# Three edits to the selective scan of a two-layer hybrid network on one core: transposing products, a folding product, and the place of the decay products

## Chip, cores and metric

One core of one Trainium2 chip. The metric is the device time of one execution in microseconds (us); three executions of the kernel before took 1320.59, 1317.4 and 1319.07 us, median 1319.07 us. Everything is float32 or a float32 split into two parts that TensorE takes in its faster float32 form.

## The reference, cut to what matters

A network of two layers works on 512 tokens (the latent stream) and 256 context tokens, 1024 channels each. Each layer normalises and modulates its input, projects it, and feeds three mixers in parallel: an attention, a long convolution and a selective scan (SSD), whose outputs are gated, joined, projected back and normalised. The second layer needs the context only as far as the latent stream reads it.

The change is inside the scan. It runs in both directions over chunks of 128 tokens, for 8 heads of 64 channels in 2 groups of 4, with a state of 128 numbers per channel. In one chunk and one direction:

```
acs      = cumsum(dt * a)                         # dt: softplus(projection + bias), per head
decay_ls = exp(acs[l] - acs[s])  for s <= l       # 128 x 128 per head
y_diag   = sum_s  (C[l] . B[s]) * decay_ls * dt[s] * x[s]
y_off    = (C[l] . state at the chunk's start) * exp(acs[l])
y        = y_diag + y_off  (both directions added)  + x * d_skip
```

## The kernel before, in words

The kernel is one long program. A scheduler in the compiler lays down a fixed order for each engine, taking ready instructions by the order in which they were written; on the chip each engine then follows its list, and waits where a semaphore tells it to. Work of different stages is therefore mixed in the list of TensorE: while the scan runs, the blocks of the input projection (`proj`, lines 450 and 452; a block is 128 output channels, and its weights come through two buffers `wr` and are split on ScalarE and VectorE, lines 170 and 171) and of the modulation (line 359) are its other work. In layer 0 the order of the steps is "V, S, 1, P, 2, G" and in layer 1 "S, V, 1, P, 2, G": `S` is `ssm_in`, `P` is `ssm`, the other letters are projections for the long convolution.

`ssm_in` (lines 669 to 759) projects x, B, C and the step sizes dt. The projection of dt is made with its weights' high and low parts side by side, so the result `dr` has 32 rows: 16 high, 16 low. Lines 704 and 705 make it, with stationary operands of 32 columns. Lines 707 to 711 then turn it round, tokens onto partitions, into `pd`: for each of 6 chunks two products with a part of the identity, the second added to the first, so that high and low parts are summed. VectorE's line 718 reads `pd` and begins a chain of small instructions to dt, its cumulative sums (lines 738 to 745), and `rd`, two rows per head in DRAM.

`ssm` (lines 761 to 845) first runs the states from chunk to chunk (`scan`, lines 772 to 792), then goes over the chunks, six in layer 0 and four in layer 1. For a chunk:

- line 798: B times C for both groups, copied by ScalarE to `gm` (line 800); lines 805 and 807 find what a token adds to itself (`own`).
- lines 810 to 819: `ys`, on VectorE: x times `own`, plus for either direction the product of C with the state (line 816, into `po`) times its decay. Tokens are on the partitions.
- line 821: four products of 128 columns each, `ys` as the stationary operand and the identity as the moving one: `ys` transposed, into the accumulator `py`, whose bank they open.
- lines 823 to 842, for each group: a tile `R` of 512 KB is loaded from `rd`, broadcast to all partitions (line 825); six bias instructions of ScalarE (line 833) and two of VectorE (line 831); a predicated copy (line 835); an exponential (line 836); and line 838, which multiplies with `gm` into a tile `M` of its own. Then four products (line 842), one per head, add the group's decay part to `py`.
- line 843 copies `py` to `bc`, line 844 stores it.

`R` has three buffers, `M` two. A buffer of `R` comes free with line 838, and that of `M` with line 842. All the loads and stores named here are issued from SyncE's queue (SP), in one order. PSUM has five banks `wk` for these products.

Of the kernel before, what the change touches and what calls it, by code (L numbers as in the profile page):

```python
# [9 lines left out]
F32 = mybir.dt.float32  # L10
# [8 lines left out]
P = 128  # L19
# [16 lines left out]
# columns of the per-layer parameter block  # L36
C_HCW, C_SCW, C_NW, C_BM = 0, 48, 80, 84
NPAR = 108
# columns of the constant block
K_ID, K_U, K_L, K_ONE = 0, 128, 256, 384  # L40
NCON = 512
# blocks of 128 columns of w_in
# [3 lines left out]
class Net:  # L46
    def __init__(self, ctx, tc, a):
        self.tc, self.nc, self.a = tc, tc.nc, a
        nc = self.nc
        self.one = ctx.enter_context(tc.tile_pool(name="one", bufs=1))  # L50
        self.dr = ctx.enter_context(tc.tile_pool(name="dr", bufs=1, space=DRAM))
        self.ps = ctx.enter_context(tc.tile_pool(name="ps", bufs=1, space=PSUM))
        self.sb = ctx.enter_context(tc.tile_pool(name="sb", bufs=1))
        self.n = 0
        self.kd = {}
        self.th = {}
        self.ph = None
        self.rr = 0

        self.ml = self.tq([P, 4, 768])  # L60
        fw = self.ml[:, 3]
        self.fw = fw
        nc.sync.dma_start(self.ml.rearrange("p a b -> p (a b)")[0:33, 1536:2432], a["mlp1"])
        self.cc = self.one.tile([P, 16], F32, name="cc")
        nc.sync.dma_start(self.cc, a["cc"])
        nc.sync.dma_start(fw[:, 128:392], a["mlp2"])
        self.row = self.one.tile([P, DEPTH, 48], F32, name="row")
        nc.sync.dma_start(self.row, a["row"].partition_broadcast(P))
        self.con = self.one.tile([P, NCON], F32, name="con")
        nc.sync.dma_start(self.con, a["con"])  # L70
        self.ident = self.con[:, K_ID:K_ID + P]
        self.par = self.one.tile([P, DEPTH, NPAR], F32, name="par")
        nc.sync.dma_start(self.par, a["par"].rearrange("l p n -> p l n"))
        self.identb = self.one.tile([P, P], BF16, name="identb")
        nc.vector.tensor_copy(self.identb, self.ident)
        self.maskb = self.one.tile([P, 2, P], BF16, name="maskb")
        mk = self.ip("V", [P, QW])[:, :2 * P]
        nc.sync.dma_start(mk, a["mask"])
        nc.vector.tensor_copy(self.maskb.rearrange("p a b -> p (a b)"), mk)
        self.upper = self.one.tile([P, P], mybir.dt.uint8, name="upper")  # L80
        nc.vector.tensor_copy(self.upper, self.con[:, K_U:K_U + P])
        gc = self.one.tile([P, 512], F32, name="gc")
        self.gc = gc.rearrange("p (q s k) -> p q s k", q=2, s=2)
        self.mhalf = self.one.tile([P, 16], F32, name="mhalf")
        nc.vector.memset(self.mhalf, -0.5)
        for l in range(DEPTH):
            s = self.par[:, l, C_SCW:C_SCW + 32]
            nc.vector.tensor_scalar_mul(s, s, 0.5)
        self.nega = self.one.tile([P, DEPTH, 16], F32, name="nega")
        self.nsink = self.one.tile([P, DEPTH, 8], F32, name="nsink")  # L90
        nc.vector.tensor_scalar_mul(self.nsink, self.row[:, :, 32:40], -1.0)
        self.sc = self.one.tile([P, 8, 32], F32, name="sc")
        nc.vector.memset(self.sc, 0.0)
        # sums over the column groups of the tensor engine
        self.sel = self.one.tile([P, 4], F32, name="sel")
        i4 = self.ident.rearrange("p (q i r) -> p q i r", q=2, i=2)[:, :, :, 0:2]
        nc.vector.tensor_tensor(self.sel.rearrange("p (i r) -> p i r", i=2), i4[:, 0], i4[:, 1], op=ALU.add)

    def vectors(self):
        """The conditioning vectors' silu and the scans' rates."""  # L100
# [23 lines left out]
    def tq(self, shape, dt=F32):  # L124
        """One of the large tiles, whose lives cross phases."""
# [7 lines left out]
    def w(self, tag, shape, dt=F32, bufs=2):  # L133
        """A working tile of the present phase."""
        return self.al(self.ph, tag, shape, dt, bufs)

    def ip(self, tag, shape, dt=F32, bufs=2):
        """A working tile of the input projection."""
        return self.al(self.sb, tag, shape, dt, bufs)
# [24 lines left out]
    def split(self, src, hi, lo, lo_on=None):  # L164
        """hi + lo = src, both fit float32r; src in PSUM for lo_on="v" alone."""
# [55 lines left out]
    def filter_mlp(self):  # L221
# [8 lines left out]
        def sine(lhsT, rhs, col_b, col_f, out, c0):  # L230
            """sin(freq * (product + bias)) for 256 tokens, reduced in turns."""
# [28 lines left out]
    def filter_tables(self, st):  # L260
        """The cosine and sine tables of one of the streams, and both streams' windows."""
# [16 lines left out]
    def filters(self, l, st):  # L278
        """Spectra of layer l's two filters for one of the streams, over its length."""
# [14 lines left out]
        for o in range(2):  # L294
# [4 lines left out]
            for sd in range(2):  # L299
# [7 lines left out]
                for t in range(NT):  # L307
# [10 lines left out]
                    if t == 0 and sd == 0:  # L318
                        # the direct term is a tap at time 0
# [3 lines left out]
                for q in range(HT):  # L323
                    ps = self.wk()

                    def sums(par):
                        """The sum over the even times, then with the odd ones' added to it."""
# [17 lines left out]
    def modulation(self, l, n, mod, big):  # L345
        """Shift, scale + 1 (as columns) or, for n = 2, gate (without its bias, as rows in DRAM) of both streams."""
# [57 lines left out]
    def norm_in(self, xt, i0, hs, mod, psum=None):  # L404
        """hs: the two [128, 1024] normalised token tiles from tile i0 on."""
# [27 lines left out]
    def proj(self, l, b, xt, both, parts=False):  # L433
# [4 lines left out]
        if parts:  # L438
            # by groups of tokens, as they come from the previous layer
# [15 lines left out]
    def gate(self, pl, pc, out):  # L455
        """2 * silu(u)"""
# [8 lines left out]
    def gate_mul(self, l, b0, j, xt, sp, both):  # L465
        """Block j of a group's output, in DRAM and halved, times 2 * silu(u); returns its tile and a free one."""
# [19 lines left out]
    def ssm_gate(self, l, xt, sp, last):  # L486
        """Also the group RMS norm's factors, to DRAM."""
# [5 lines left out]
        for g in range(2):  # L493
# [7 lines left out]
            # sums over the channels, with the tokens on the partitions  # L501
# [38 lines left out]
    def att_in(self, l, xt, last):  # L540
# [8 lines left out]
        # keys twice, high part over low part  # L549
# [27 lines left out]
    def att(self, l, q, ks, vt, last):  # L577
        """Attention's output takes the place of q, halved, and goes to DRAM."""
        nc = self.nc
        sp = self.dr.tile([4, P, QW], F32, name=self.nm("sp"))  # L580
        for n in list(range(4)) + ([] if last else [4, 5]):
            lat = n < 4
            q0 = n * P if lat else n * P + 1
            # the window's blocks, then the context's; an inner block's own keys come last, in a bank of their own
# [84 lines left out]
    def ssm_in(self, l, xt, last):  # L669
# [23 lines left out]
        # dt: the 16 columns, high and low parts side by side  # L693
# [14 lines left out]
        i2 = self.con[0:32, K_ID:K_ID + 32].rearrange("p (a b) -> p b a", a=2)  # L708
        for c in range(6):
            for i in range(2):  # L710
                nc.tensor.matmul(pd[:, c * 16:(c + 1) * 16], lhsT=dr[0:32, c * P:(c + 1) * P], rhs=i2[:, :, i], start=i == 0, stop=i == 1)
        # layout (dir, chunk, head)
# [36 lines left out]
        # X: dt * decay to the end; Z: exp(acs); S: exp(total)  # L749
# [5 lines left out]
        # S2: log(dt) - acs  # L755
# [5 lines left out]
    def ssm(self, l, xT, bt, bc, sc, rd, last):  # L761
        """The scans' output takes the place of B and C, halved, and goes to DRAM."""
# [31 lines left out]
        for c in (0, 1, 2, 3) if last else (4, 5, 0, 1, 2, 3):  # L794
# [6 lines left out]
            # what a token adds to itself: the skip term and the reversed scan's diagonal  # L801
# [18 lines left out]
            for j in range(4):  # L820
                nc.tensor.matmul(py[:, j * P:(j + 1) * P], lhsT=ys[:, j * P:(j + 1) * P], rhs=self.ident, start=j == 0, stop=False, skip_group_check=True)
            # within the chunk: dt * decay, forward above the diagonal and on it, reversed below
            for g in range(2):
                R = self.w("R", [P, 2, 4, P], bufs=3)
# [12 lines left out]
                M = self.w("M", [P, 4, P], bufs=2)  # L837
                nc.vector.tensor_tensor(M, E, gm[:, g].unsqueeze(1).to_broadcast([P, 4, P]), op=ALU.mult)
                for h in range(4):
                    hh = 4 * g + h  # L840
                    r0, j = 64 * (hh % 2), hh // 2
                    nc.tensor.matmul(py[r0:r0 + 64, j * P:(j + 1) * P], lhsT=xT[:, c, 64 * hh:64 * hh + 64], rhs=M[:, h], start=False, stop=True, skip_group_check=True)
# [5 lines left out]
    def hy_in(self, l, xt, last, b0, fill, x2s):  # L848
# [3 lines left out]
        for j in range(4):  # L852
# [12 lines left out]
            if b0 == B_HV:  # L865
                # folded about the middle: sums and differences, even places first
# [8 lines left out]
    def fold(self, v, f, c0, L):  # L875
        """f's place: v's second half plus and minus its first, reversed."""
# [7 lines left out]
    def hy(self, l, spill, last):  # L884
# [4 lines left out]
        for o in range(2):  # L889
            for st in range(1 if last else 2):  # L890
# [3 lines left out]
                for hf in range(2):  # L894
                    # fold about the middle, then turn: [time, (sum, difference), 256 channels]
# [82 lines left out]
    def out(self, l, cats, rsd, gd, hsrc, done, last):  # L978
# [17 lines left out]
        def weights(k):  # L996
            """Split rows of w_out; as many as fit are kept for the groups to come."""
# [17 lines left out]
        def pieces(i0, i):  # L1015
            """The columns of a token tile as they are finished."""
            return ((0, 512), (512, 256), (768, 256)) if last and i0 + i == 3 else ((0, 512), (512, 512))

        def mul(gi, i0):
# [35 lines left out]
            if final:  # L1055
                # one accumulator after the other: the epilogue of the first ones runs beside the last
# [163 lines left out]
def _constants():  # L1220
# [18 lines left out]
    # all indices of the long transform go even ones first  # L1239
# [42 lines left out]
def _layout(i):  # L1282
    """The inputs, laid out for the loads."""
# [61 lines left out]
```

## Time and profile before

| | |
|---|---|
| three executions | 1317.4 to 1320.59 us, median 1319.07 us |
| span of the profiled execution | 1314.3 us; the page shows no time of its own beside it |
| PE (TensorE products) busy | 1248.2 us, 95% |
| PEld (weight loads, beside PE) busy | 989.3 us, 75% |
| DVE (VectorE), ACT (ScalarE), POOL (GpSimd) busy | 954.1, 591.9, 130.4 us |
| DMA | 208.94 MB, mean 159 GB/s |

The span runs from the first to the last instruction on the chip; the median is 4.8 us above it. A busy figure is the union of the engine's instructions. A float32 product is a pair of records in the trace, so four products of line 821 are eight records; records of a matmul overlap, so what one costs its engine is read from one start to the next, not from its duration. "PEclk" in a window is the clock that was granted to TensorE: 1.00 is 2.4 GHz, 0.50 is 1.2 GHz.

### The profile page before, as it was taken

What the parts mean: (1) busy time and instruction counts of PE and PEld (TensorE: products, weight loads), DVE (VectorE), ACT (ScalarE), POOL (GpSimd) and SP (SyncE); (2) the same over time, 40 slices, a digit from 0 to 9 for tenths busy, and PEclk for the clock granted to TensorE, in tenths of its full rate; (3) what the DMA queues carried; (4) which work ended last, traced back from release to release, by engine and by line L of the source; (5) the groups of instructions that cost most, each with busy time, mean ns of one, the idle gap of its engine ahead of it and who ended that gap; (6) DMA issues with size and microseconds to landing.
All of it is one profiled execution on the core that took longest, in us unless ns stands there. A gap on an engine that the chain in (4) does not pass through costs nothing.

```text
span 1314.3 us, 19207 instructions
## 1 busy us (share of the span) xinstructions
PE 1248.2 (95%) x6942; PEld 989.3 (75%) x6942; DVE 954.1 (73%) x1962; ACT 591.9 (45%) x1151; POOL 130.4 (10%) x117
## 2 busy tenths in 40 slices
PE   5997999999999989999999998999999999899997
PEld 3564887766877777799988777786677687798886
DVE  7889548768556786389846899777677688497676
ACT  5567516646234264333234454455544626343340
POOL 2332010000000000012110232100000000011102
PEclk9999899999998999999989999999999999999999
DMA  6777333112315466854479852441111726855872
GB/s 228 257 269 241 123 112 104 55 33 67 119 59 149 153 182 201 299 184 126 152 236 295 263 191 106 116 114 44 33 57 73 257 71 173 277 170 176 262 251 80
DMA packets 109192, 208.94 MB, mean 159 GB/s; under 512 B 10553, under 2 KB 55033, under 8 KB 109096
## 3 DMA queue, kind: packets, MB, share of 16 engines
q1 hardware_dynamic: 109096, 207.70, 49.7%
q8 instruction: 55, 0.90, 0.3%
q14 instruction: 41, 0.34, 0.1%
HBM read 162.44 MB, written 38.41 MB: 153 GB/s over the span
## 4 chain that ended last, share of the span: by engine, by line
PE 53%; DVE 16%; DMA 11%; issue 10%; ACT 6%; POOL 2%; SPq 1%; POOLq 0%; DVEq 0%; ACTq 0%
PE pl L450 18%; PE pc L452 7%; PE wk L663 4%; PE wk L175 3%; PE wk L177 3%; PE wk L176 3%; PE wk L654 3%; DMA R<-rd 3%; DMA wr<-in_tab_dram 2%; PE wk L622 1%; DMA Q<-in_w_mod_dram 1%; DMA wo<-in_w_out_dram 1%; ACT wh L170 1%; DVE wl L171 1%; DMA wr<-in_fwo_dram 1%
## 5 line engine op out<-in xcount | busy, mean ns | idle before, releaser
L450 PE MATMUL pl<-Q,wh 128*128 128x512 f32 x1168 | 407.4, 403 | 0.0
L450 PEld LDWEIGHTS pl<-Q,wh 128*128 128x128 f32 x1168 | 217.6, 189 | 54.2 <-issue 6.4
L450 PE MATMUL pl<-Q,wl 128*128 128x512 f32 x584 | 232.8, 399 | 0.0
L452 PE MATMUL pc<-Q,wh 128*128 128x256 f32 x704 | 179.4, 291 | 0.3 <-DVE V L463 0.3
L170 ACT ACTIVATE wh<-wr 128x1024 fp32r<-128x1024 f32 x76 | 80.4, 1057 | 183.5 <-PE pc L452 121.3
L452 PEld LDWEIGHTS pc<-Q,wh 128*128 128x128 f32 x704 | 126.8, 193 | 9.4 <-issue 2.7
L450 PEld LDWEIGHTS pl<-Q,wl 128*128 128x128 f32 x584 | 110.3, 189 | 23.6 <-issue 0.8
L171 DVE TENSOR_TENSOR wl<-wr,wh 128x1024 fp32r<-128x1024 f32 x76 | 100.6, 1325 | 35.5 <-ACT wh L170 35.2
L932 POOL TENSOR_TENSOR ta<-ta 128x256 f32<-128x256 f32 x40 | 32.0, 799 | 760.3 <-DVE ta L930 460.0
L452 PE MATMUL pc<-Q,wl 128*128 128x256 f32 x352 | 101.4, 288 | 0.0
L452 PEld LDWEIGHTS pc<-Q,wl 128*128 128x128 f32 x352 | 67.9, 193 | 0.6
L663 PE MATMUL wk<-pt,vt 128*64 128x512 f32 x160 | 60.7, 615 | 0.2 <-DVE pt L659 0.2
L654 PEld LDWEIGHTS wk<-con,pr 128*128 128x128 f32 x320 | 35.8, 141 | 29.8 <-issue 19.9
L632 DVE TENSOR_REDUCE S<-wk 128x1 f32<-128x512 f32 (+1 forms) x80 | 49.4, 631 | 11.7 <-PE wk L631 9.1
L659 DVE COPY pt<-wk 128x512 f32<-128x512 f32 x50 | 33.4, 688 | 31.6 <-PE wk L654 31.3
L634 ACT ACTIVATE pr<-wk,S 128x512 f32<-128x512 f32 (+1 forms) x80 | 51.2, 646 | 7.4 <-DVE S L633 7.2
L833 ACT ACTIVATE R<-R,sc 128x128 f32<-128x128 f32 x120 | 38.6, 391 | 26.3 <-DMA R<-rd 25.2
L654 PE MATMUL wk<-con,pr 128*128 128x128 f32 x320 | 48.8, 279 | 0.0
L170 ACT ACTIVATE wh<-wo 128x1024 fp32r<-128x1024 f32 x30 | 31.6, 1056 | 34.8 <-DMA wo<-in_w_out_dram 13.4
L171 DVE TENSOR_TENSOR wl<-wo,wh 128x1024 fp32r<-128x1024 f32 x30 | 38.7, 1292 | 9.5 <-ACT wh L170 9.5
L175 PE MATMUL wk<-ph,Q 128*128 128x256 f32 x144 | 40.6, 294 | 4.9 <-ACT ph L170 4.9
L170 ACT ACTIVATE yh<-ta 128x512 fp32r<-128x512 f32 x32 | 20.2, 631 | 54.4 <-DVE ta L933 54.2
(393 smaller groups left out, 2929.8 us busy)
## 6 DMA issues: line engine op xcount, KB each, us to landing
wr<-in_w_in_dram SPq DMA_DIRECT2D x76, 512.0 KB, 3.8
Q<-in_w_mod_dram SPq DMA_DIRECT2D x24, 1024.0 KB, 7.3
wo<-in_w_out_dram SPq DMA_DIRECT2D x43, 512.0 KB, 5.5
kd<-k SPq DMA_DIRECT2D x40, 256.0 KB, 2.7
R<-rd SPq DMA_DIRECT2D x20, 512.0 KB, 6.1
kt<-kd SPq DMA_DIRECT2D x40, 256.0 KB, 3.1
sp<-V SPq DMA_DIRECT2D x20, 384.5 KB, 3.9
cs<-sp SPq DMA_DIRECT2D x60, 128.0 KB, 4.1
```

The costliest lines, as they stand in the source:

```text
L170: nc.scalar.activation(hi, src, AF.Copy)
L171: (nc.gpsimd if lo_on == "p" else nc.vector).tensor_tensor(lo, src, hi.bitcast(F32), op=ALU.subtract)
L175: mm(out, lhsT=lh, rhs=rh, start=start, stop=False, **k)
L176: mm(out, lhsT=lh, rhs=rl, start=False, stop=False, **k)
L177: mm(out, lhsT=ll, rhs=rh, start=False, stop=stop, **k)
L450: nc.tensor.matmul(pl, lhsT=w[:, k * P:(k + 1) * P], rhs=x[:, 0:SEQ], start=s, stop=e)
L452: nc.tensor.matmul(pc[:, 0:CTX], lhsT=w[:, k * P:(k + 1) * P], rhs=x[:, SEQ:SEQ + CTX], start=s, stop=e)
L632: nc.vector.tensor_reduce(m[:, h:h + 1], sa[:, :wa], axis=AX.X, op=ALU.max)
L634: nc.scalar.activation(pr[:, h, :wa], sa[:, :wa], AF.Exp, bias=negm[:, h:h + 1], scale=0.125, accum_out=sums[:, h:h + 1])
L654: nc.tensor.transpose(ps[:, h * P:(h + 1) * P], prs[g][:, h, i * P:(i + 1) * P], self.ident)
L663: nc.tensor.matmul(pv[r0:r0 + 64], lhsT=vt[:, keys[i], r0:r0 + 64], rhs=pt[g], start=i == 0, stop=i == nk - 1)
L833: nc.scalar.activation(R[:, d, h], R[:, d, h], AF.Identity, bias=bias)
```

## The change

It replaces the two folding products per chunk by one, with a constant made once; it runs line 821 in TensorE's transposing mode; it writes the decay into the first half of `R` in place of `M`, gives `R` a fourth buffer, and issues the decay products of both groups behind each other, group 1 first, with an ordering edge that keeps group 0's behind the first of group 1's. It also drops comments, which moves line numbers. Shown here without them:

```diff
+        self.fold16 = self.one.tile([P, 16], F32, name="fold16")[0:32]
+        nc.vector.tensor_tensor(self.fold16, self.ident[0:32, 0:16], self.ident[0:32, 16:32], op=ALU.add)
...
+    def after(self, later, earlier):
+
+        self.tc.add_manual_dep(later.ins, earlier.ins.name, mybir.DependencyInfo(mybir.DependencyClass.NoSync, mybir.DependencyReason.DATA), reason="order")
...
-        i2 = self.con[0:32, K_ID:K_ID + 32].rearrange("p (a b) -> p b a", a=2)
         for c in range(6):
-            for i in range(2):
-                nc.tensor.matmul(pd[:, c * 16:(c + 1) * 16], lhsT=dr[0:32, c * P:(c + 1) * P], rhs=i2[:, :, i], start=i == 0, stop=i == 1)
+            nc.tensor.matmul(pd[:, c * 16:(c + 1) * 16], lhsT=dr[0:32, c * P:(c + 1) * P], rhs=self.fold16, start=True, stop=True)
...
             for j in range(4):
-                nc.tensor.matmul(py[:, j * P:(j + 1) * P], lhsT=ys[:, j * P:(j + 1) * P], rhs=self.ident, start=j == 0, stop=False, skip_group_check=True)
+                nc.tensor.matmul(py[:, j * P:(j + 1) * P], lhsT=ys[:, j * P:(j + 1) * P], rhs=self.ident, start=j == 0, stop=False, is_transpose=True, skip_group_check=True)
+            Ms = []
             for g in range(2):
-                R = self.w("R", [P, 2, 4, P], bufs=3)
+                R = self.w("R", [P, 2, 4, P], bufs=4)
...
-                M = self.w("M", [P, 4, P], bufs=2)
+                M = R[:, 0]
                 nc.vector.tensor_tensor(M, E, gm[:, g].unsqueeze(1).to_broadcast([P, 4, P]), op=ALU.mult)
-                for h in range(4):
-                    hh = 4 * g + h
-                    r0, j = 64 * (hh % 2), hh // 2
-                    nc.tensor.matmul(py[r0:r0 + 64, j * P:(j + 1) * P], lhsT=xT[:, c, 64 * hh:64 * hh + 64], rhs=M[:, h], start=False, stop=True, skip_group_check=True)
+                Ms.append(M)
+            mm = {}
+            for hh in (4, 5, 6, 7, 0, 1, 2, 3):
+                r0, j = 64 * (hh % 2), hh // 2
+                mm[hh] = nc.tensor.matmul(py[r0:r0 + 64, j * P:(j + 1) * P], lhsT=xT[:, c, 64 * hh:64 * hh + 64], rhs=Ms[hh // 4][:, hh % 4], start=False, stop=True, skip_group_check=True)
+            for hh in range(4):
+                self.after(mm[hh], mm[4])
```

## Rows read from the trace of the kernel before

**Rows 1.** The page, busy time, share of the span and instructions of each engine.
```profile
PE 1248.2 (95%) x6942; PEld 989.3 (75%) x6942; DVE 954.1 (73%) x1962; ACT 591.9 (45%) x1151; POOL 130.4 (10%) x117
```
**Rows 2.** The page, chain that ended last, shares by engine.
```profile
PE 53%; DVE 16%; DMA 11%; issue 10%; ACT 6%; POOL 2%; SPq 1%; POOLq 0%; DVEq 0%; ACTq 0%
```
**Rows 3.** Windows: length, then PE, PEld, DVE, ACT, POOL; granted clock, DMA share, GB/s.
```profile
457.00:512.00 55.00, 49.46 (x337) 39.75 (x335) 45.60 (x117) 31.86 (x80) 0.00 (x0) 1.00 0.55 153
1081.00:1116.00 35.00, 32.91 (x205) 26.17 (x204) 31.05 (x71) 21.74 (x52) 0.00 (x0) 1.00 0.57 156
...
978.00:981.00 3.00, 3.00 (x20) 2.56 (x20) 2.87 (x7) 0.60 (x1) 0.00 (x0) 1.00 0.81 240
385.00:394.00 9.00, 9.00 (x56) 6.11 (x54) 5.88 (x8) 3.30 (x5) 0.00 (x0) 1.00 0.18 58
394.00:401.00 7.00, 7.00 (x27) 6.02 (x27) 3.70 (x18) 0.28 (x1) 0.00 (x0) 0.51 0.00 0
```
**Rows 4.** Waits: waiter and releaser, us in total, times, longest us.
```profile
PE wk L842 <- DVE M L838: 5.4, 3, 2.2
...
PE wk L821 <- DVE ys L819: 2.2, 3, 1.5
...
SPq L825 <- DVE M L838: 26.0, 11, 6.8
```
**Rows 5.** Instructions of lines 821, 842 and 680, whole trace: ns min/median/max.
```profile
L821 PE MATMUL wk<-con,ys x80: 270/275/377, 459.2 to 1111.4; 128*128 128x128 f32 x80
...
L680 PE MATMUL wk<-con,V x48: 270/273/329, 326.9 to 980.0; 128*128 128x128 f32 x48
...
L842 PE MATMUL wk<-M,Q x160: 272/273/324, 460.2 to 1115.3; 128*64 128x128 f32 x160
```
**Rows 6.** PE's timeline in the scan and in the projection of x: start, us.
```profile
459.18 1.05 PE L821 MATMUL wk<-con,ys 128*128 128x128 f32 x8
460.17 1.09 PE L842 MATMUL wk<-M,Q 128*64 128x128 f32 x16
461.19 0.71 PE L798 MATMUL wk<-Q 128*128 128x128 f32 x4
...
481.62 0.66 PE L842 MATMUL wk<-M,Q 128*64 128x128 f32 x8 [1.47 <-DVE M L838]
482.21 0.49 PE L798 MATMUL wk<-Q 128*128 128x128 f32 x2
484.36 0.66 PE L842 MATMUL wk<-M,Q 128*64 128x128 f32 x8
...
978.74 1.49 PE L680 MATMUL wk<-con,V 128*128 128x128 f32 x12
979.98 0.71 PE L450 MATMUL pl<-Q,wh 128*128 128x512 f32 x2
```
**Rows 7.** PE's timeline around the folding products, layer 0.
```profile
392.06 1.95 PE L711 MATMUL wk<-con,V 32*128 32x16 f32 x16
393.94 0.59 PE L450 MATMUL pl<-Q,wh 128*128 128x512 f32 x1
...
394.89 1.88 PE L711 MATMUL wk<-con,V 32*128 32x16 f32 x8
396.71 0.80 PE L452 MATMUL pc<-Q,wh 128*128 128x256 f32 x2
```
**Rows 8.** SP's timeline, layer 0: issues of R for the third and fourth chunk.
```profile
462.40 0.45 SPq L825 DMA_DIRECT2D R<-rd  x1
...
466.02 0.36 SPq L825 DMA_DIRECT2D R<-rd  x1
...
473.01 0.36 SPq L825 DMA_DIRECT2D R<-rd  x1
...
481.60 2.78 SPq L825 DMA_DIRECT2D R<-rd  x2
```
**Rows 9.** The page, DMA issues: count, KB each, median us to landing.
```profile
R<-rd SPq DMA_DIRECT2D x20, 512.0 KB, 6.1
```

## The prediction

> **What bounds the kernel now.** I read the busy times first: PE is busy for 1248.2 of 1314.3 us [rows 1], so 66 us of the whole span are not PE's. The chain that ended last says the same more mildly: 53% of it is PE, and DVE, DMA and others share the rest [rows 2]. Then the stretches where the change acts. In layer 0 the loop over the chunks fills about 457 to 512 us, in layer 1 1081 to 1116 us [rows 3]. PE is busy for 49.46 of 55 and 32.91 of 35 us there, DVE for 45.60 and 31.05. So PE leads, but it stands idle for 5.5 + 2.1 = 7.6 us, and DVE has only 9.4 and 4.0 us to spare: if PE got much faster, DVE would be the next to bind. The waits name nearly the whole of PE's idle time in the loops: 5.4 us for the decay tile M and 2.2 us for ys [rows 4]. Last comes the timeline of PE, which gives the price of each product, from one start to the next, in the parts below.
>
> **Transposed terms.** The eighty records of line 821 [rows 5] are ten chunks of four products, two records each. One chunk's eight take from 459.18 to 460.17, 0.99 us, 0.248 us a product [rows 6]. What the changed line will do is already in the trace: line 680 makes transposes of the same float32 size, one record each. Twelve of them take from 978.74 to 979.98, 1.24 us, 0.103 us each [rows 6]. So 40 products save 0.145 us each, 5.8 us. The bounds: nothing, if a transpose into an accumulator that others add to is done like a product, and 5.8 us. I take 5.8, as operands and shape are those of line 680; only the accumulator differs. PE has other work queued behind them, so what they free is used.
>
> The Trainium skill ("TensorE: Matmul & The Clock Gate", Terms) calls the transposing mode 4 times faster for float32. The trace shows 0.248 / 0.103 = 2.4 times; by the page the term would be 40 x 0.186 = 7.4 us, an estimate, and the time 1.6 us lower.
>
> **The fold.** Sixteen records of line 711 take from 392.06 to 393.94, 1.88 us, and the other eight from 394.89 to 396.71, 1.82 us [rows 7]. The eight cost twice as much each because the clock is then at its lower level: 0.51 in the mean of 394 to 401, after 1.00 in 385 to 394 [rows 3]. At the full clock a record is 1.88 / 16 = 0.118 us, and 24 of them 2.8 us. Half go, in both layers: 2.8 us. PE is busy without a gap from 385 to 401 [rows 3], and the removed products are in the middle of that, so this is taken from the path. The new constant costs one DVE instruction of 32 x 16 elements in the setup; it is not on any path named here, and uncovered it would cost about as much as a small DVE instruction, well under 1 us. I count nothing.
>
> **The clock near the fold.** Before it fell, PE had run the narrow products of lines 704 and 705 (32 columns of weights) and then the first sixteen records of line 711. The half level costs 0.9 us on the second group of line 711 (1.82 - 0.94) and half of most of the remaining 5 us, about 3.1 us together. With half the records the narrow work is shorter by 1.4 us, so the fall may not come; or it may come all the same, as most of the narrow work stays. The bounds are 0 and 3.1 us. I take 0, as most of the narrow work stays. It might also fall in layer 1, where it did not: a loss of the same 3.1 us.
>
> **One stretch of decay products.** Where both groups are issued together, sixteen records take from 460.17 to 461.19, 1.02 us; a group alone takes from 481.62 to 482.21, 0.59 us, so two alone 1.18 [rows 6]. That is 0.16 us a chunk. Two of the ten chunks are together already; eight give 1.3 us. The bound from below is 0.
>
> **Waits.** This edit adds a wait: group 0's products now stand behind group 1's M. Behind them on PE wait the next chunk's lines 798 and 816 and the projection's blocks; ACT's line 843, and DVE's line 818 of the next chunk, wait for these. Between the two groups' products of one chunk there are 2.7 us now (481.62 to 484.36) [rows 6], and I price all eight split chunks by it. But PE does lines 798 and 816 or a block in that time, and none of it needs the decay products, so it can go in front of the joined stretch. In exchange one of two places to wait disappears, and the loads of R go out earlier. Before, R has three buffers, and SP waits 26.0 us for M to free one [rows 4]: the third chunk's loads leave at 462.40 and 466.02, the fourth's at 473.01 and 481.60 [rows 8]. After, the fourth buffer is loaded long ahead, so the second chunk can finish without the wait for its second tile. Buffers now come free with the joined stretch: the third chunk's two at about 461.2, when the first chunk's products end [rows 6], and the fourth's some 8 us later, near 469. That is 1 to 13 us earlier than now, on a chain that begins with 6.1 us of transfer [rows 9]. The transfers are as many as before; none is added to SP's or POOL's queue. The memory of M pays for the buffer. M written into R costs DVE the same instruction.
>
> So the 7.6 us of idle time can shrink, but DVE's spare time sets a limit, and an order fixed beforehand will still meet tiles that are late: bounds from a gain of all 7.6 to a loss, at 2.7 us for each of eight chunks, of 21.6 us. I take a gain of 2, near the small end, since both PE and DVE are close to full. What is late next is ys and the second M, both by DVE.
>
> **Sum.** 5.8 + 2.8 + 1.3 + 2 = 11.9 us: a span of 1302.4 in place of 1314.3. The profiled span lies 4.8 us under the median of the runs, and I take that distance as fixed: 1319.07 - 11.9 = 1307.2 us.
>
> **Rivals.**
> - *All of it works* (16 in 100). The loads come so early that the waits for M and ys vanish, and the clock holds: 9.9 + 7.6 + 3.1 = 20.6 us, 1298.5 us. For it: two waits account for the idle time. Against: DVE is at 83 and 89% in the loops [rows 3].
> - *Given back* (11 in 100). The pace of the loop is DVE's, with R's transfer, and PE merely waits longer: the 7.1 us of the loop's products turn into idle time, and half the fold too, as its chain on DVE goes on. 1.4 us remain, 1317.7 us. Against it: in the loops PE is fuller than DVE in both layers, and work of the projection fills its gaps.
> - *The joined stretch stalls PE* (6 in 100). At the eight chunks, PE reaches group 1's first product with nothing left to put ahead, and stands for the 2.7 us that now lie between the groups: 21.6 us lost, 9.9 gained, 1330.8 us. It decides when more than half of those gaps (9.9 / 2.7, four chunks) are unfilled. Against it: today only 5.4 us are waited for M in all [rows 4].
> - *Transposes cost what products cost* (4 in 100): the change does less than it says, and 5.8 us stay: 1313.0 us.
> - *The clock falls after the transposes* (2 in 100). If each of ten chunks lost 3.1 us as at 394 to 401, the sum would be 31 - 11.9 = 19 us slower, 1338 us. Against it: twelve transposes in a row, amid wide products, ran at 1.00 from 978 to 981 [rows 3]. The Trainium skill ("TensorE: Matmul & The Clock Gate", Part 4) says that transposes do not count as PE being busy for the full clock. By that rule this case would be the likely one; a chunk has only four, 0.4 us, between wide products, and the trace speaks against it.
>
> **The numbers.** The forecast has 61 in 100. A measurement of this kernel can tell about 0.2%, 2.6 us, from no change. Faster by more than that: forecast, all works, transposes dear, 61 + 16 + 4 = 81. Within it: given back, 11. Slower: the stall and the clock, 8. The range reaches from the full gain, 1298, to 1317, just short of the given-back case, and leaves out that case and the two slower ones, 19 in 100.
>
> **What would show it.** Right: line 821 has forty records, four of them in about 0.4 us; line 711 has 24; line 842 stands in ten groups of sixteen records; PE's busy time is lower by about 10 us, and its idle time in the two loops is under 7.6 us; R's third pair leaves SP near 461. Wrong: PE's busy time falls but its idle time rises by as much, at line 842 or 821 or after the loops; the loops take longer than 55 and 35 us; a clock at 0.50 in the loops or near line 711 in layer 1; eighty records at line 821.

## The result, and the profile after

The change makes the kernel slower: 1325.79 us in the median of five executions (1324.04 to 1332.35), beside 1319.07 us (1317.29 to 1321.86) for five of the kernel before in the same session. The ratio is 1.0062, with an interval of 1.0039 to 1.0085. The forecast of 1307.2 us is missed by 18.6 us, and its range ends 8.8 us too low. The profiled execution took 1324.04 us and spans 1322.3 us, 8.0 more than the span before. That is somewhat more than the medians differ, since the profile before was of a quick execution (mean granted clock 0.988; 0.984 is the mean of 111 later ones).

The page's busy times come first.

```profile
PE 1247.3 (94%) x6878; PEld 985.7 (75%) x6878; DVE 957.6 (72%) x1963; ACT 591.9 (45%) x1151; POOL 134.1 (10%) x117
```

PE runs 64 records less than in [rows 1], which is 40 of the transposed terms and 24 of the fold, but it is busy for only 0.9 us less; the clock, below, is one reason. The instructions of the three lines that the change edits follow (count, then minimum, median and maximum in ns, first and last start in us).

```profile
L827 PE MATMUL wk<-con,ys x40: 270/273/447, 461.5 to 1121.4; 128*128 128x128 f32 x40
L717 PE MATMUL wk<-fold,V x24: 257/258/278, 397.7 to 1015.5; 32*128 32x16 f32 x24
L851 PE MATMUL wk<-R,Q x160: 272/273/477, 462.2 to 1122.5; 128*64 128x128 f32 x160
```

Line 827 is line 821 of before, 717 is 711 and 851 is 842 [rows 5]. The maxima of 447 and 477 ns are records at the lower clock. The windows show where that lies (length, then PE, PEld, DVE, ACT, POOL; granted clock, DMA share, GB/s).

```profile
457.00:520.00 63.00, 54.61 (x350) 43.80 (x349) 49.36 (x123) 31.13 (x78) 0.00 (x0) 0.92 0.60 152
...
385.00:394.00 9.00, 9.00 (x48) 6.50 (x47) 5.18 (x9) 3.43 (x4) 0.00 (x0) 1.00 0.24 72
394.00:401.00 7.00, 7.00 (x48) 5.47 (x46) 4.12 (x13) 1.16 (x2) 0.00 (x0) 1.00 0.16 59
...
500.00:510.00 10.00, 5.99 (x34) 4.71 (x34) 7.84 (x21) 3.13 (x9) 0.00 (x0) 0.83 0.45 108
510.00:520.00 10.00, 9.04 (x56) 6.83 (x57) 5.74 (x14) 3.35 (x5) 0.00 (x0) 0.66 0.34 113
```

At the fold the clock stays at 1.00 where it had fallen to 0.51 [rows 3]. In the loop over the chunks it is the other way round: 1.00 before, 0.92 now, with PE busy for only 5.99 of ten microseconds from 500 on. The waits (waiter and releaser, us in total, times, longest) name what PE stood for.

```profile
ACT R L840 <- DMA R<-rd: 32.4, 13, 4.7
...
PE wk L827 <- DVE ys L825: 10.7, 5, 3.6
```

The 7.6 us for M and ys [rows 4] have become 10.7 us for ys alone. ScalarE waits 32.4 us for the loads of R; in the kernel before, where its line is 833, it was 25.2:

```profile
ACT R L833 <- DMA R<-rd: 25.2, 15, 5.5
```

The timeline of PE in layer 0's loop (start, us) shows both the gain and the new wait.

```profile
470.29 0.60 PE L827 MATMUL wk<-con,ys 128*128 128x128 f32 x4
470.82 1.09 PE L851 MATMUL wk<-R,Q 128*64 128x128 f32 x16
471.85 0.71 PE L804 MATMUL wk<-Q 128*128 128x128 f32 x4
...
481.34 0.63 PE L827 MATMUL wk<-con,ys 128*128 128x128 f32 x4 [1.48 <-DVE ys L825]
...
490.42 0.63 PE L827 MATMUL wk<-con,ys 128*128 128x128 f32 x4 [0.80 <-DVE ys L825]
...
501.40 1.09 PE L827 MATMUL wk<-con,ys 128*128 128x128 f32 x4 [2.54 <-DVE ys L825]
502.42 1.98 PE L851 MATMUL wk<-R,Q 128*64 128x128 f32 x16
...
510.96 0.63 PE L827 MATMUL wk<-con,ys 128*128 128x128 f32 x4 [3.58 <-DVE ys L825]
```

A chunk's four transposes take 0.53 us instead of 0.99 [rows 6], and sixteen decay products 1.03. But the chunks follow each other no faster: from 461.46 to 501.40, four chunks, 10.0 us each; in the kernel before the transposed terms start at 459.18 [rows 6] and 498.65, 9.9 us each.

```profile
498.65 1.16 PE L821 MATMUL wk<-con,ys 128*128 128x128 f32 x8 [1.54 <-DVE ys L819]
```

What sets the change's pace is read from its SP timeline (R is a load of line 832, sp the store of a finished chunk).

```profile
462.91 0.38 SPq L832 DMA_DIRECT2D R<-rd  x1
463.99 0.37 SPq L855 DMA_DIRECT2D sp<-Q  x1
464.44 0.46 SPq L832 DMA_DIRECT2D R<-rd  x1
...
471.52 0.36 SPq L832 DMA_DIRECT2D R<-rd  x1
474.74 0.36 SPq L855 DMA_DIRECT2D sp<-Q  x1
475.19 0.46 SPq L832 DMA_DIRECT2D R<-rd  x1
...
482.60 0.36 SPq L832 DMA_DIRECT2D R<-rd  x1
484.79 0.36 SPq L855 DMA_DIRECT2D sp<-Q  x1
485.20 0.50 SPq L832 DMA_DIRECT2D R<-rd  x1
...
491.89 0.36 SPq L832 DMA_DIRECT2D R<-rd  x1
496.60 0.36 SPq L855 DMA_DIRECT2D sp<-Q  x1
497.01 0.50 SPq L832 DMA_DIRECT2D R<-rd  x1
```

A chunk's first load leaves when the joined products have freed a buffer (471.52, behind those from 470.82). Its second load stands in SP's list behind the store of the chunk just done, and leaves 1.5 to 5.1 us after the first. ScalarE's timeline shows why the store is late.

```profile
492.75 1.86 ACT L840 ACTIVATE R<-R,sc 128x128 f32<-128x128 f32 x6 [3.42 <-DMA R<-rd]
...
495.99 0.58 ACT L854 ACTIVATE Q<-wk 128x512 f32<-128x512 f32 x1
496.47 0.36 ACT L806 ACTIVATE gm<-wk 128x256 f32<-128x256 f32 x1
```

The copy that the store waits for (line 854) stands behind bias instructions that wait 3.42 us for a load of R themselves; so a late load makes the next one later. (It is the load that left at 485.20, the fifth chunk's second; the copy is the fourth chunk's, whose products had started on PE at 491.20.) Behind them stands the next chunk's `gm` too (line 806), and from there VectorE's timeline leads to PE's wait:

```profile
496.87 0.29 DVE L811 SCALAR_TENSOR_TENSOR dg<-gm,con 128x128 f32<-128x128 f32 x1 [1.41 <-ACT gm L806]
...
500.56 0.69 DVE L825 TENSOR_TENSOR ys<-ys,yo 128x512 f32<-128x512 f32 x1
```

`ys` is finished at 501.25, and PE, idle for 2.54 us, starts its transposes at 501.40, at half the clock: these four take 1.02 us.

### The profile page after: what moved, and what is told of

It is laid out like the page before. It is cut to its first block, busy times and chain, and to the rows that moved or that the text cites. A ratio compares the mean times of both kernels' runs of the same rounds, so it can differ in the third digit from the quotient of the medians.

```text
span 1322.3 us, 19088 instructions
## 1 busy us (share of the span) xinstructions
PE 1247.3 (94%) x6878; PEld 985.7 (75%) x6878; DVE 957.6 (72%) x1963; ACT 591.9 (45%) x1151; POOL 134.1 (10%) x117
## 5 line engine op out<-in xcount | busy, mean ns | idle before, releaser
L840 ACT ACTIVATE R<-R,sc 128x128 f32<-128x128 f32 x120 | 37.6, 390 | 32.4 <-DMA R<-rd 32.4
L180 PE MATMUL wk<-plo,Q 128*128 128x256 f32 x144 | 40.5, 285 | 0.8 <-DVE plo L175 0.7
```

Of the source, the lines that this page charges most:

```text
L180: mm(out, lhsT=lh, rhs=rl, start=False, stop=False, **k)
L840: nc.scalar.activation(R[:, d, h], R[:, d, h], AF.Identity, bias=bias)
```

## Experiments

Each kernel is the one before with one or more parts of the change, or the change with one part undone. Ratios are to executions of the kernel before in the same session; its medians there were 1321.12, 1322.36, 1321.47 and 1321.13 us.

**The fold and its constant.** The constant alone, its result not used by anything:

```diff
+        self.fold16 = self.one.tile([P, 16], F32, name="fold16")[0:32]
+        nc.vector.tensor_tensor(self.fold16, self.ident[0:32, 0:16], self.ident[0:32, 16:32], op=ALU.add)
```

> The kernel before with nothing but the folding constant made in the setup (one more VectorE instruction, result not used). Theory 1, the instruction reorders the setup in the compiled lists, and that costs what the changed kernel was late by before its scan began: slower by 4 to 6 us, about 1324 us, and the block of products that ended at 384.8 us in the profile before ends near 390. Rival, the changed kernel's late start was the clock's luck in one profile: within 2 us of before.

Measured: 1324.26 us, ratio 1.0027, 1.0003 to 1.0051. One small instruction costs about 3 us, less than the 4 to 6 expected. The compiler lays the setup's work down in another order beside it. One visible sign is the load of dt's weights in SP's timeline, in the kernel before and here:

```profile
99.93 0.33 SPq L695 DMA_DIRECT2D dw<-in_w_dt_dram  x1
...
47.74 0.33 SPq L697 DMA_DIRECT2D dw<-in_w_dt_dram  x1
```

Another is that dt's narrow products (line 704 of before) begin at 390.04 us here and at 391.07 in the change, in place of 385.40. With the same constant made at its first use (change_const_late, below) the load stands at 99.31 and the narrow products at 385.42. So the instruction's place costs, and not its work; which of the moves costs the time was not separated.

The fold with the constant made where it is first used:

```diff
         for c in range(6):
-            for i in range(2):
-                nc.tensor.matmul(pd[...], lhsT=dr[...], rhs=i2[:, :, i], start=i == 0, stop=i == 1)
+            if l == 0 and c == 0:
+                self.fold16 = ...
+            nc.tensor.matmul(pd[...], lhsT=dr[...], rhs=self.fold16, start=True, stop=True)
```

> The kernel before with the single folding product, its constant written down where it is first used, so that the compiled lists of all engines keep the order of before but for one VectorE instruction. Theory: 2.8 to 4.4 us faster, about 1315 us, 24 records of the folding product, everything before 385 us at the time of before. Rival, the products gained there are waited away in the scan behind: within 1 us of before.

Measured: 1314.73 us, ratio 0.9961, 0.9937 to 0.9985: 5.2 us gained. The profile of the change agrees. From dt's first narrow product to the modulation behind the fold, with twelve records of PE fewer between them, layer 0 took 19.8 us (385.40 to 405.20) and takes 15.4 (391.07 to 406.44): 4.4 us quicker. In layer 1, from the same product to line 738's (744 of the change), it is 1.3 us. That is half of 2.8 us in each, and in layer 0 the 3.1 us of the half clock too. The fall of the clock is not the same in every kernel, though. Of the eight profiles with two products per chunk six have it in layer 0 at 385 to 410 us, with 3.4 or 6.8 us at half the clock, and the one before is among the longest; of the ten with one product none has it.

**The transposes.** Alone, and then with the fold as above (the second kernel was run again later):

```diff
-... rhs=self.ident, start=j == 0, stop=False, skip_group_check=True)
+... rhs=self.ident, start=j == 0, stop=False, is_transpose=True, skip_group_check=True)
```

> The kernel before with the transposing mode alone. Theory 1, the transposes do what they should and the trouble in the scan comes from the joined stretch and its loads: 3 to 6 us faster, 1313 to 1316 us, both scan loops no longer than 55 and 35 us. Theory 2, the transposes themselves upset the scan (the clock falls after them, or the list is ordered worse): no gain or slower by up to 4 us, with half clock in the loops.

> The fold (constant written at its first use) and the transposing mode, with the loop's loads, tiles and decay products as before. Theory 1, these two parts each save about 2.5 us of span at equal clock and do not disturb each other: 5 us less span times clock than before (1297.8), about 1293, and a median of 1311 to 1317 us, faster than before. Rival, the transposing mode's gain is always lost again in later waits and a lower clock: no faster than the fold alone (1314.7 us), or slower.

> The kernel fold_and_transpose once more, beside fold_trans_four: both theories expect its ratio of 0.9938 again, within 0.002, some 1310 to 1316 us.

Measured: alone 1319.91 us, 0.9992 (0.9964 to 1.0020); with the fold 1312.87 us, 0.9938 (0.9918 to 0.9958), and again 1313.98 us, 0.9956 (0.9931 to 0.9982). Beside the fold's 0.9961 the transposes are worth some 0.05 to 0.2%, 1 to 3 us, and alone they can't be told from nothing. The chunk's row above has the gain (0.46 us, ten times); what is lost again isn't one wait, and the expectation for the transposes alone, 3 to 6 us faster, was missed. In the run of the transposes alone PE still waits for M, a little longer than the 5.4 us of [rows 4]:

```profile
PE wk L842 <- DVE M L838: 5.9, 4, 2.2
```

**The joined stretch and the fourth buffer.** All of the change's loop edit but the transposing; the same without joining (four buffers, M in R, products by group); and the joined stretch alone (three buffers of R, M in two of its own).

```diff
-                R = self.w("R", [P, 2, 4, P], bufs=3)
+                R = self.w("R", [P, 2, 4, P], bufs=4)    # joined_only, held_split
-                M = self.w("M", [P, 4, P], bufs=2)
+                M = R[:, 0]                              # joined_only, held_split
...
-                for h in range(4): ...                   # joined_only, stretch_three
+            for hh in (4, 5, 6, 7, 0, 1, 2, 3): ...
```

> The kernel before with the joined stretch, four buffers of R and M written into R, nothing else. Theory 1, group 1's load of R stands behind the store of a chunk's result in SyncE's list, which waits for ScalarE, which waits for group 0's load: slower by 3 to 6 us, 1322 to 1325 us, with PE waiting for ys in the loop of layer 0 and a chunk taking 9 to 11 us there. Theory 2, the loss is the transposes': faster by 1 to 3 us.

> The kernel before with four buffers of R and M written into R, but each group's decay products issued on their own as before (no joined stretch). Theory 1a, what costs is that a buffer of R is given back only after TensorE's products: like joined_only, 1327 to 1333 us. Theory 1b, what costs is the joined stretch: within 2 us of before (1321.1 us).

> The kernel before with the joined stretch alone: M in its own two buffers, R in three, given back at M as before. Theory 1a, holding R is what costs: within 2 us of before, 1319 to 1323 us. Theory 1b, the stretch costs: like joined_only, 1327 to 1333 us.

Measured: 1331.16 us, 1.0076 (1.0048 to 1.0105); 1335.23 us, 1.0091 (1.0070 to 1.0111); and 1319.80 us, 0.9983 (0.9967 to 0.9999). Without the transposes the products' place alone harms nothing. With M in R the kernel loses 0.8 to 0.9%, joined or not, more than the 1322 to 1325 us expected of the joined one. The waits of the second kernel, whose products stand where they stood before, show the picture of the change:

```profile
ACT R L833 <- DMA R<-rd: 32.3, 15, 5.8
...
PE wk L821 <- DVE ys L819: 10.8, 5, 3.9
```

**The holding alone.** The change with one line undone, which leaves four buffers of R and the joined stretch; and the same pair with the constant at its first use.

```diff
-                M = R[:, 0]
+                M = self.w("M", [P, 4, P], bufs=2)       # change_m_own, best_four_buffers
```

> The change with one line undone: M in a tile of its own, two buffers, R still in four; the constant stays in the setup. Theory (holding costs some 10 us): a ratio to the kernel before of 0.994 to 1.000, some 1314 to 1321 us, and the loads of R leave before the store of the chunk ahead. Rival (holding is not it, the joined stretch is, as best_three_buffers was slow without any holding): 1.004 to 1.008, as the change.

> The whole change, its constant made at its first use in layer 0's scan input and not in the setup. Theory: the constant alone cost about 3.1 us (1324.26 against 1321.12 us), by the order that the compiler makes of the setup, so the change should lose about that: a ratio to the kernel before of 1.000 to 1.004, some 1320 to 1326 us at before's median of these sessions; what stays is the held buffers of R. Rival: beside the other edits the constant's place is worth nothing, and the ratio stays at the change's 1.005 to 1.008. Line 821's wait for ys should stay near 10 us by both.

> The kernel best_three_buffers with a fourth buffer of R and nothing held: M keeps its own two buffers, R is free with the multiplication into M. Theory (it is the holding that costs, not the number of buffers): as fast as best_three_buffers within 0.3%, or faster by up to 0.3%, as R's loads leave a little earlier; ACT's wait for R at or under before's 25 us. Rival (a fourth buffer by itself puts group 1's load behind the chunk's store in SP's list): 0.5 to 0.9% slower than best_three_buffers, with a PE wait for ys near 10 us.

Measured: 1317.63 us, 0.9986 (0.9962 to 1.0010), beside the change's 1.0062; and 1315.15 us, 0.9956 (0.9939 to 0.9973), beside 1325.81 us, 1.0038 (1.0019 to 1.0057) with M in R. Holding costs 0.76 and 0.82%, some 10 us. A lower clock of the whole execution is not the reason: the mean granted clock is 0.9814 with M in R and 0.9815 without in the first pair, 0.9823 and 0.9825 in the second. The constant costs 0.24 and 0.30% between these same kernels, as it did alone. SP's timeline of the first:

```profile
460.57 0.38 SPq L832 DMA_DIRECT2D R<-rd  x1
463.90 0.37 SPq L855 DMA_DIRECT2D sp<-Q  x1
464.36 0.45 SPq L832 DMA_DIRECT2D R<-rd  x1
...
467.86 1.63 SPq L832 DMA_DIRECT2D R<-rd  x2
...
479.45 1.56 SPq L832 DMA_DIRECT2D R<-rd  x2
483.70 0.36 SPq L855 DMA_DIRECT2D sp<-Q  x1
...
488.67 1.56 SPq L832 DMA_DIRECT2D R<-rd  x2
```

From the fourth chunk on both loads of a chunk now leave within 1.6 us, ahead of the store: at 467.86 in place of 471.52 and 475.19, at 479.45 in place of 482.60 and 485.20, at 488.67 in place of 491.89 and 497.01. ScalarE's wait for R is 23.1 us and PE's for ys 4.8. The chunks' transposes show the pace, four chunks in 36.05 us, 9.0 us each:

```profile
461.38 0.60 PE L827 MATMUL wk<-con,ys 128*128 128x128 f32 x4
...
497.43 0.60 PE L827 MATMUL wk<-con,ys 128*128 128x128 f32 x4
```

Layer 0's loop can be measured between two products of the projection that stand on either side of it in these three kernels (in the change line 458 ahead of four products of line 788, and the last record of line 460). Windows from the start of the one to that of the other, for the kernel before, the change and the change with M apart:

```profile
453.62:526.04 72.42, 66.77 (x447) 52.48 (x446) 53.10 (x132) 36.06 (x86) 0.00 (x0) 1.00 0.61 181
...
455.89:531.32 75.43, 67.04 (x424) 52.76 (x422) 53.33 (x130) 34.02 (x80) 0.00 (x0) 0.93 0.64 168
...
455.81:523.25 67.44, 63.56 (x423) 50.80 (x422) 52.97 (x130) 34.25 (x80) 0.00 (x0) 0.97 0.61 189
```

That is 75.4 us against 67.4 us; the kernel before takes 72.4. Eight microseconds are in this one loop, and not all of them are waiting. PE is idle for 8.4 us in the one and 3.9 in the other, all of it for ys: 4.5 us. The other 3.5 us are PE's own, for the same work: 10.3 us of the change's loop are at half the clock, and 3.4 with M apart. Against the kernel before, the change's span is 2.3 us behind when this loop starts, loses 3.0 in it and 2.7 after it.

One caution holds for all these pairs: with each edit the compiler lays the lists down anew. ScalarE runs ten bias instructions in a row from 476.01 us with M apart, and six there in the change. So a pair can differ by more than its edited line.

**The order on SP.** The same loop edits with the chunk's store issued from ScalarE, so that no load stands behind it; and M in R with a fifth buffer instead.

```diff
-            nc.sync.dma_start(sp[...], bc[...])
+            nc.scalar.dma_start(sp[...], bc[...])        # joined_store_act, change_store_act
```

> As joined_only, with the store of a chunk's result issued from ScalarE in place of SyncE, so that no load of R stands behind it. Theory 1, the order of loads and stores on SyncE makes the loop slow: 4 to 8 us faster than joined_only (1331.2 us), 1323 to 1327 us, and group 1's loads leave together with group 0's. Rival, R is held too long whatever the queue: within 2 us of joined_only.

> The change with the chunk's store issued from ScalarE's queue and not from SP's; M still in R. Theory (a held buffer costs because group 1's load then stands behind the store in SP's list): about 6 us faster than the change, as joined_store_act against joined_only, a ratio of 0.999 to 1.003, and the loads of R leave in pairs within 1 us. Rival (the buffer is late in any case, the store only passes in the meantime): within 2 us of the change, 1.004 to 1.008.

> M written into R, products by group as before, R in five buffers instead of four. Theory: a held buffer is one buffer less for the loads, so a fifth gives back what holding took: the loads leave earlier, ACT's wait for R falls from 32 to about 25 us, the ratio from 1.0091 to 0.999 to 1.003. Rival (the order on SP decides, and a load stays behind a store at any count): a store stays between a chunk's two loads, the ratio stays over 1.005.

Measured: 1324.69 us, 1.0021 (0.9997 to 1.0046), beside 1.0076; 1323.66 us, 1.0018 (0.9999 to 1.0037), beside 1.0062; and with five buffers 1326.55 us, 1.0048 (1.0032 to 1.0065), beside 1.0091. SP's timeline of the change with the store on ScalarE:

```profile
469.68 0.87 SPq L832 DMA_DIRECT2D R<-rd  x2
...
481.21 1.21 SPq L832 DMA_DIRECT2D R<-rd  x2
...
490.98 0.87 SPq L832 DMA_DIRECT2D R<-rd  x2
```

The pairs are together again, and 0.44 and 0.55% come back, over half of what holding costs. The rest stays: the pairs leave when PE's products are done, later than at 467.86, 479.45 and 488.67. The fifth buffer gives half back, 0.43%, less than the first theory expected; ACT's wait for R did fall, to 26.3 us. In its list, too, no store stands between a chunk's two loads from the fourth chunk on. So both the late release and the store's place cost, and these runs do not say which is the larger.

**Can the parts be had without the cost?** Fold, transposes and the joined stretch with three buffers of R and nothing held; and fold and transposes with a fourth buffer, products by group.

> The fold with its constant at first use, the transposes, and the joined stretch with M in two buffers of its own and R in three. Theory: each part that gained alone is kept (0.9938 for fold and transposes together, 0.9983 for the joined stretch) and the held buffer is left out, so 0.990 to 0.994, 1308 to 1314 us, and a wait of PE for ys of 1 to 3 us. Rival: the joined stretch gives nothing beside the transposes, a ratio of 0.994 to 0.998, or a loss over 0.998.

> The kernel fold_and_transpose with a fourth buffer of R: products by group, M in its own two buffers. Theory (the joined stretch is worth little): within 0.2% of fold_trans_again, or up to 0.3% faster as the loads leave earlier. Rival (a fourth buffer alone harms, or helps by more than the whole joined stretch): over 0.3% from it.

Measured: 1329.19 us, 1.0067 (1.0042 to 1.0092), a clear miss; and 1310.49 us, 0.9920 (0.9892 to 0.9949), the fastest kernel of the study. The waits of the slow one:

```profile
PE wk L826 <- DVE ys L824: 6.5, 4, 2.5
PE wk L849 <- DVE M L844: 6.3, 4, 2.6
```

With three buffers a joined stretch finds the second M late; with four, best_four_buffers has no such row, and is 1.1% faster, where its theory allowed at most 0.3% and its rival expected it slower. It looks like the forecast's rival of the stalled joined stretch, with the fourth buffer as the cure. But stretch_three waited nearly as long for M (5.9 us) and lost nothing. Why the stretch with three buffers cost 1.1 to 1.3% beside the transposes was not separated; its mean clock was lower too, 0.979, and its layer 0 has 13.6 us at half the clock between 457 and 535 us, the most of all profiles. The other kernel, with products by group, lies 0.36% under fold_trans_again, just past its rival's mark of 0.3%, but their intervals overlap.

**The change as a chain of kernels**, each ratio to the kernel before (the mean of the two runs for the second):

| kernel | ratio | step |
|---|---|---|
| fold, constant at first use | 0.9961 | -0.39% |
| and transposes | 0.9947 | -0.14% |
| and joined stretch, fourth buffer | 0.9956 | +0.09% |
| and M in R | 1.0038 | +0.82% |
| and the constant in the setup (the change) | 1.0062 | +0.24% |

The first and the fourth step stand clear of their intervals; the last is supported by the three comparisons together; the second and third are within the uncertainty. The third can be split: the fourth buffer alone brings the ratio to 0.9920, and the joined stretch on top of it back to 0.9956; these two intervals overlap as well.

## Why the prediction was wrong

- **Waits: the step that failed.** "Buffers now come free with the joined stretch ... That is 1 to 13 us earlier than now", and so a gain of 2 us. It counted the fourth buffer and treated its later release as harmless. It weighed only when the loads leave, chunk by chunk, against the kernel before. There it was nearly right: 461.2 and near 469 were forecast for the third and fourth chunk, 462.91 and 471.52 came, in a loop that starts some 2 us later. But each chunk's second load slips behind a store and leaves up to 5.1 us after the first, and ScalarE's list, made for four buffers, asks for the loads sooner: ahead of the third chunk's copy it has the bias instructions of both of the fourth chunk's groups, where before it had only the first group's. The release has moved from DVE to PE, and PE waits for `ys`, behind those loads. So the pace stays at 10.0 us a chunk in place of the 8 us assumed from 461 to 469. With the same four buffers and M apart it is 9.0. The holding is worth about +10 us, and the two loops have waits of 10.7 us for ys where under 7.6 in all were forecast. The +10 us lie inside the stated bound of 21.6, by another mechanism than the one the bound was worked out from.
- "None is added to SP's or POOL's queue" was true and beside the point. No DMA was added, but the place of the chunk's store between its loads on SP was not looked at, and over half of what holding costs came back when the store was moved.
- **The constant:** "I count nothing" was wrong by about 3 us. The instruction is small; the new order of the setup was not a cost that the forecast considered.
- **The fold:** right, and more. 2.8 us of products were taken away, and the fall of the clock beside them didn't come: the upper bound of that term, 3.1 us, was nearer the truth in layer 0 of these two profiles than the 0 taken. With 5.2 us measured it is the largest gain.
- **Transposes:** the price was nearly right on the engine (0.53 us a chunk, 0.46 saved, 4.6 in ten chunks against 5.8 forecast), and the rival that they cost what products cost is out. The term was mis-sized in the time, 1 to 3 us. The Trainium skill ("TensorE: Matmul & The Clock Gate", Terms) has the mode 4 times faster for float32; here it is 0.99 / 0.53, 1.9 times.
- **The clock rival** ("falls after the transposes"), at its price of 3.1 us for every chunk, is not what happened. In the change five of layer 0's six chunks run their transposes in 0.60 to 0.63 us, at the full clock; held_split and joined_only have no transposing at all and a lower mean clock (0.980) than transpose_only (0.982). A smaller form of it stays open. In the change's two loops (457 to 535 and 1081 to 1125 us) PE has 13.7 us at half the clock, about 6.8 us lost, and the kernel before has none: no term of the sum stood for this. So PE's busy time in layer 0's loop is 67.0 us beside 66.8 before, and over the whole kernel it fell by 0.9 us and not by the forecast's 10. In the same two windows of all profiles, one per kernel, there are 3.8 us at half the clock in the mean of the eight without transposing (0 to 10.2) and 7.5 us in that of the ten with it (3.4 to 13.7). The falls at 501 and 511 us stand behind PE's waits of 2.54 and 3.58 us and at its transposes; which of the two brings them was not separated.
- **One stretch of decay products:** a chunk's sixteen do take 1.03 us. With a gain of 1.3 us forecast, stretch_three measured 0.17%, 2.2 us; with the fold and transposes in place nothing is left of it, and with three buffers it costs.
- The rival on the slower side, 1330.8 us, came nearest in time but had the wrong place: PE stalls at ys, for want of loads, and not at group 1's product.
- The distance of 4.8 us between span and median, taken as fixed, is that of a quick execution. An execution's own time is 1.7 to 1.8 us above its span in every later profile (1324.04 beside 1322.3 for the change). The forecast is a difference, so this did not move it.

## What to carry to other kernels

Writing a result into the tile that it was made from saves memory but no instruction, and moves that tile's release to the last reader of the result. If the tile is filled by a DMA, ask who releases it now, whether that engine itself waits for the next fill, and what stands between the two fills in the issuing queue. Here a fourth buffer did not make up for a release that had been put behind the bottleneck, and a fifth made up for half; and a small instruction added to a compiler-scheduled setup is not free until it is measured.

## What the runs showed of the hardware that was not expected

Executions of one kernel differ by more than the fold is worth: 111 of the kernel before took from 1311.59 to 1327.23 us. The time follows the mean granted clock of the execution (0.978 to 0.990), 9.2 us for 0.01 in a straight line through them (correlation -0.76). The mean clock was 0.984 for the kernel before, 0.981 for the change and 0.980 for the two kernels that hold R without the fold. In the change's loop, 500 to 520 us at 0.83 and 0.66 is 10 us at half the clock, 5 us lost, in a stretch that ran at 1.00 before. That such a fall follows from the waits was not shown: with less than half of the wait for ys, change_m_own has the same mean clock as the change.
